# Forty-six of forty-eight input columns by seven block products, with heads that go through DRAM

## The chip, the core and the metric

The kernel runs on one core of a Trainium2 chip. The core has five engines that work side by side, each through its own queue of instructions in order: TensorE (PE in the profile) multiplies matrices, VectorE (DVE), ScalarE (ACT) and GpSimd (POOL) work element by element, and SyncE (SP) issues most of the DMA transfers. An instruction starts when the one ahead of it in its queue is done and the semaphores that it waits for have their values. The metric is the time in microseconds (us) of one execution on the device.

## What is computed

One layer of a hybrid encoder on 576 frames (512 of a prompt, 64 that continue a running stream of 512 cached frames), in float32, with 2048 channels:

```python
hn = rmsnorm(x, g_norm1)
q, k, v, gb, gc, hc = split(hn @ w_in)            # 2048 -> 6 x 1024 columns
q, k = rmsnorm(q per head, g_q), rmsnorm(k per head, g_k)
# attention, 8 heads x 128: A[t,s] = beta_ts * prod_{s<j<t}(1 - beta_tj), s < t
z = q @ k.T / sqrt(128)
log_1mb = where(s < t, log_sigmoid(-z), 0)
after = reversed_cumsum(log_1mb) - log_1mb
o_attn = where(s < t, exp(log_sigmoid(z) + after), 0) @ v
u = gc * hc                                       # convolution of width 3 along the frames
o_conv = gb * (w0*u[t-2] + w1*u[t-1] + w2*u[t])
x = x + concat(rmsnorm(o_attn, g_attn), rmsnorm(o_conv, g_conv)) @ w_out
h2 = rmsnorm(x, g_norm2)
x = x + (silu(h2 @ w_gate) * (h2 @ w_up)) @ w_down     # 2048 -> 5632 -> 2048
```

The normalised keys, the values and the last two rows of u are outputs too.

## The kernel before

Channels lie on the 128 partitions and frames along the free dimension, so every projection is a sum over 16 slices `k` of 128 channels of (128x128 weights) x (128x288 frames); the 576 frames are two halves of 288. Each operand is split in two float32r parts, hi and lo, and each slice takes three matmuls: hi x hi, lo x hi, hi x lo. ScalarE makes a hi part by a cast and VectorE the lo part by a subtraction; of 1024 columns of weights that is a pair of instructions (`split`, `weight_parts`).

A plain column chunk (128 of the 6144 columns of `w_in`) therefore takes 16 x 3 x 2 = 96 matmuls (`project`, `product`, tile "pj", L211). All 48 chunks are plain: three for each head (q, k, v), then three for each of the eight conv groups. x is transposed at the start into the tile `x_all` and also written to DRAM, since the residual needs it again.

For gate, up and down the kernel already uses the other scheme, a seven-product form of 2x2 block multiplication: a unit covers 256 columns by 2048 channels as blocks a11, a12, a21, a22, with the frames in blocks as well. `weight_sums` makes three sums and differences of weight blocks and `prepare` splits the operand of a product, four products ahead of its use, into one of four buffers `whl`. `run` does a product (24 matmuls over eight slices) and hands results on. A unit takes 7 x 24 = 168 matmuls where two plain chunks take 192.

Only PE's order is that in which the code is written; on the other engines a scheduler orders most instructions, except where the code asks for the written order (the start, and the last part). Small work on PE is interleaved by a queue of generators, `Pipeline`: a tick comes after each slice (three matmuls), and a generator that yields n is resumed n ticks later. So `attend`, the attention of a head, issues its pieces between slices of the projection that runs at the time, and a number behind `yield` says how much PE work lies between two pieces.

One head in `attend` is this chain. PE makes three blocks of scores z (the pieces z2, z1, z0) and the scores of the 64 sample frames against the cache (zs). ScalarE and VectorE form softplus of each block (three ScalarE activations and one VectorE instruction), GpSimd masks, and the result is split into hi and lo. PE then applies a triangular matrix to these parts (a cumulative sum) in z itself, and for the sample frames in the tile `cz`, from the split parts `sph` and `spl`; ScalarE takes exp; PE multiplies by v (tiles `po`, `os`). Before the change these pieces lie 15 to 18 ticks apart, and a head takes three chunks, 96 ticks.

After the heads and the conv groups `make_mix` normalises the two groups of channels, and the output projection follows, the attention half of `w_out` first, then the conv half with `after_b2`, which forms what the gate and up stage needs. Gate, up and down take up the rest of the time and are not touched by the change.

Of the kernel before, what the change touches and what calls it, by code (L numbers as in the profile page):

```python
# [16 lines left out]
P = 128  # L17
# [32 lines left out]
)  # L50

# [42 lines left out]
def tile_hybrid_stream_step(  # L94
# [21 lines left out]
    tmp = ctx.enter_context(tc.tile_pool(name="tmp", bufs=2, side="left"))  # L116

    lpad = ctx.enter_context(tc.tile_pool(name="lpad", bufs=1, side="left"))
    lpad.tile([P, 8], F32, name="lpad_t")
    rpad = ctx.enter_context(tc.tile_pool(name="rpad", bufs=1, side="right"))  # L120
    rpad.tile([P, 56], F32, name="rpad_t")
    acon = tc.alloc_tile_pool(name="acon", bufs=1, side="left")
    xt_dram = tc.dram_tile([KD, P, T], F32, name="xt_dram")
    x2_dram = tc.dram_tile([KD, P, T], F32, name="x2_dram")
    hid_dram = tc.dram_tile([NFP, 2 * FORMS, P, HALF], F32, name="hid_dram")
    ps_pj = ctx.enter_context(tc.tile_pool(name="ps_pj", bufs=3, space=PSUM))


    specs = []

    def col_chunk(w, col):
        specs.append((w[:, col : col + P].rearrange("(k p) c -> p k c", p=P), KD, P))

    for h in range(NH):
        for j in range(3):
            col_chunk(w_in, j * AW + h * P)
    for g in range(NG):
        for j in (1, 2, 0):
            col_chunk(w_in, 3 * AW + j * CW + g * P)
    for half in range(2):  # L140
        for c in range(D // 256):
            specs.append((w_out[half * AW : (half + 1) * AW, c * 256 : (c + 1) * 256]
                          .rearrange("(k p) c -> p k c", p=P), NH, 256))
# [5 lines left out]
    UNITS = [(kind, fp, 0, NP) for fp in range(1, NFP) for kind in ("gate", "up")]  # L149
    NGU = len(UNITS)  # L150
    calls = down_calls()
    UNITS += [("down", d, a, b - a) for d, a, b in DOWN]
# [37 lines left out]
    def next_weight():  # L190
# [5 lines left out]
        while len(ready) < min(i + 2, end):  # L196
            split_weight(nc.gpsimd if i == 2 else nc.vector)
# [8 lines left out]
    def half_of(x_, k, a, b):  # L206
        return x_[:, k, a // HALF, :] if len(x_.shape) == 4 else x_[:, k, a:b]

    def step(ps, whi, wlo, csl, xhi, xlo, k, nk, a, b):
        for n, (w_, x_) in enumerate(((whi, xhi), (wlo, xhi), (whi, xlo))):  # L210
            mm(ps, w_[:, k, csl], half_of(x_, k, a, b), start=(k == 0 and n == 0), stop=(k == nk - 1 and n == 2))  # L211

    def product(ps, whi, wlo, csl, xhi, xlo, nk, a, b):
        for k in range(nk):
            step(ps, whi, wlo, csl, xhi, xlo, k, nk, a, b)
# [6 lines left out]
    def parts(name):  # L222
        t = tmp.tile([P, 2, HALF], F32R, tag="hl", name=name)
        return t[:, 0], t[:, 1]
# [4 lines left out]
    onef = acon.tile([P, P], F32, name="onef")  # L229
    nc.vector.memset(onef, 1.0)  # L230
    oner = const.tile([P, P], F32R, name="oner")
    nc.vector.tensor_copy(oner, onef)
    neg1r = acon.tile([P, P], F32R, name="neg1r")
    nc.vector.tensor_scalar(out=neg1r, in0=onef, scalar1=-1.0, scalar2=None, op0=ALU.mult)
    neg1f = acon.tile([P, P], F32, name="neg1f")
    nc.vector.memset(neg1f, -1.0)
    trif = acon.tile([P, P], F32, name="trif")
    nc.gpsimd.affine_select(out=trif, in_=neg1f, compare_op=ALU.is_ge, fill=0.0, base=0,
                            pattern=[[-1, P]], channel_multiplier=1)
    trir = acon.tile([P, P], F32R, name="trir")  # L240
    nc.vector.tensor_copy(trir, trif)
    m01 = acon.tile([P, P], F32, name="m01")
    nc.gpsimd.affine_select(out=m01, in_=onef, compare_op=ALU.is_ge, fill=0.0, base=-1,
                            pattern=[[1, P]], channel_multiplier=-1)
    mneg = acon.tile([P, P], F32, name="mneg")
    nc.vector.tensor_scalar(out=mneg, in0=m01, scalar1=-NEG, scalar2=NEG, op0=ALU.mult, op1=ALU.add)
# [1152 lines left out]
```

## Time and profile before

| | us |
|---|---|
| median of three runs | 2439.27 (2436.69 to 2440.55) |
| the profiled execution: its own span | 2438.7 |
| PE busy | 2412.2 |
| DVE busy | 1736.5 |
| ACT busy | 1086.4 |
| POOL busy | 244.8 |

The profiled span is 0.6 us under the median, so no part of the time lies outside it that matters here. In lists of groups the columns are line, engine, operation, out<-in, shapes and count, then busy time and mean nanoseconds of one, then the idle time of the engine ahead of them and what ended it. A single matmul shows about twice its share, because two are in flight; what one costs is read from counts over a busy stretch. In timelines the columns are the start, the duration, and the instruction, with idle time ahead of it in brackets. In window tables each engine has its busy time and count, then come the clock granted to PE (1.00 is full), the share of DMA time and GB/s.

### The profile page before, as it was taken

To read this page: it belongs to the slowest core of one execution; us is meant where nothing else is said; L and a number is where in the kernel's file an instruction comes from. 1 tells how busy PE (TensorE), PEld (TensorE's weight loads), DVE (VectorE), ACT (ScalarE), POOL (GpSimd) and SP (SyncE) were. 2 spreads that over 40 slices of the span, in tenths; PEclk is the share of its full clock that TensorE was granted. 3 is DMA by queue.
4 is the path that set the end of the run, shared out by engine and by line. 5 is a ranking of instruction groups with operands and counts; after the bars stand their busy time and mean duration, and the time that the engine had idled before them with its cause. 6 is when DMAs were issued, how large, how long until landed. Compare 5 with 4: busy or idle time off the path is not lost.

```text
span 2438.7 us, 44038 instructions
## 1 busy us (share of the span) xinstructions
PE 2412.2 (99%) x18137; PEld 2403.7 (99%) x18137; DVE 1736.5 (71%) x2627; ACT 1086.4 (45%) x1929; POOL 244.8 (10%) x349
## 2 busy tenths in 40 slices
PE   8999999999999999999999999999999899999998
PEld 8999999999999999999999999999999899999998
DVE  7766666363335456888888888888888777887875
ACT  6655555241122245444444444444444444444454
POOL 2110101110010021000000000000000001431211
PEclk9999999999999999999999999999999999999999
DMA  8232232222234233443544444434544845885642
GB/s 263 85 102 84 76 92 78 82 84 85 79 93 155 97 125 100 148 152 114 159 151 131 140 143 148 144 122 154 156 127 144 310 153 171 240 233 193 202 126 79
DMA packets 464530, 336.49 MB, mean 138 GB/s; under 512 B 10191, under 2 KB 456521, under 8 KB 464329
## 3 DMA queue, kind: packets, MB, share of 16 engines
q1 hardware_dynamic: 459160, 326.90, 42.5%
q0 software_dynamic: 5168, 6.79, 1.5%
q8 instruction: 142, 2.33, 0.4%
q14 instruction: 60, 0.48, 0.1%
HBM read 269.33 MB, written 64.31 MB: 137 GB/s over the span
## 4 chain that ended last, share of the span: by engine, by line
PE 95%; DVE 2%; ACT 1%; DMA 0%; issue 0%; POOL 0%; SPq 0%; POOLq 0%; ACTq 0%; DVEq 0%
PE psy L1155 33%; PE pj L211 24%; PE psw L1155 17%; PE pjo L211 8%; PE psx L1155 8%; PE z L552 1%; PE pw L998 1%; PE po L618 1%; PE pot L1306 0%; PE os L648 0%; PE zs L578 0%; DVE whl L220 0%; DVE wlo L172 0%; ACT whi L171 0%; PE pjz L211 0%
## 5 line engine op out<-in xcount | busy, mean ns | idle before, releaser
L211 PE MATMUL pj<-x_all,whi 128*128 128x288 f32 x3008 | 627.0, 297 | 2.5 <-DVE x_all L347 1.7
L211 PEld LDWEIGHTS pj<-x_all,whi 128*128 128x128 f32 x3008 | 492.5, 189 | 3.6 <-DVE x_all L347 1.9
L211 PE MATMUL pj<-x_all,wlo 128*128 128x288 f32 x1504 | 444.9, 296 | 0.1
L1155 PE MATMUL psy<-t,whl 128*128 128x288 f32 x2916 | 438.6, 295 | 0.5 <-ACT part L1165 0.5
L1155 PE MATMUL psy<-h_s,whl 128*128 128x288 f32 x2724 | 411.5, 295 | 6.3 <-ACT part L1165 6.3
L1155 PEld LDWEIGHTS psy<-t,whl 128*128 128x128 f32 x2916 | 403.6, 189 | 0.9 <-ACT part L1165 0.7
L1155 PEld LDWEIGHTS psy<-h_s,whl 128*128 128x128 f32 x2724 | 378.6, 189 | 6.6 <-ACT part L1165 6.5
L1155 PE MATMUL psw<-t,whl 128*128 128x288 f32 x2592 | 377.1, 295 | 0.0
L1155 PEld LDWEIGHTS psw<-t,whl 128*128 128x128 f32 x2592 | 354.4, 189 | 0.2
L220 DVE TENSOR_TENSOR whl<-raw_a,whl 128x1024 fp32r<-128x1024 f32 (+4 forms) x288 | 309.5, 1075 | 61.5 <-ACT whl L219 60.1
L219 ACT CAST whl<-raw_a 128x1024 fp32r<-128x1024 f32 (+4 forms) x288 | 259.6, 902 | 109.8 <-issue 35.1
L211 PEld LDWEIGHTS pj<-x_all,wlo 128*128 128x128 f32 x1504 | 283.3, 188 | 0.8 <-DVE wlo L172 0.4
L220 DVE TENSOR_TENSOR whl<-raw_b,whl 128x1024 fp32r<-128x1024 f32 (+5 forms) x186 | 196.6, 1058 | 69.2 <-ACT whl L219 68.3
L171 ACT CAST whi<-raw_a 128x1024 fp32r<-128x1024 f32 (+1 forms) x138 | 140.1, 1031 | 233.3 <-PE pj L211 95.6
L219 ACT CAST whl<-raw_b 128x1024 fp32r<-128x1024 f32 (+5 forms) x186 | 161.1, 867 | 159.7 <-issue 69.8
L1165 ACT COPY part<-psy 128x288 f32<-128x288 f32 x237 | 94.8, 400 | 281.0 <-PE psy L1155 278.8
L172 DVE TENSOR_TENSOR wlo<-raw_a,whi 128x1024 fp32r<-128x1024 f32 (+1 forms) x132 | 160.9, 1231 | 25.6 <-ACT whi L171 24.3
L1155 PE MATMUL psx<-h_s,whl 128*128 128x288 f32 x1122 | 166.6, 296 | 2.3 <-DVE gs L978 2.3
L1155 PEld LDWEIGHTS psx<-h_s,whl 128*128 128x128 f32 x1122 | 155.7, 190 | 2.5 <-issue 2.5
L219 ACT CAST whl<-s 128x1024 fp32r<-128x1024 f32 (+5 forms) x79 | 70.1, 888 | 96.6 <-PE psw L1155 94.3
L941 POOL DMA_DIRECT2D hid_dram<-form x3 | 2.4, 807 | 922.6 <-DVE form L220 922.6
L220 DVE TENSOR_TENSOR whl<-s,whl 128x1024 fp32r<-128x1024 f32 (+5 forms) x79 | 80.6, 1020 | 14.7 <-ACT whl L219 14.4
(378 smaller groups left out, 3526.6 us busy)
## 6 DMA issues: line engine op xcount, KB each, us to landing
raw_a<-in_w_in_dram SPq DMA_DIRECT2D x47, 1024.0 KB, 5.5
hid_dram<-form SPq DMA_DIRECT2D x147, 288.0 KB, 2.3
raw_a<-in_w_gate_dram SPq DMA_DIRECT2D x23, 1024.0 KB, 5.7
raw_a<-in_w_up_dram SPq DMA_DIRECT2D x23, 1024.0 KB, 6.0
raw_b<-in_w_gate_dram SPq DMA_DIRECT2D x21, 1024.0 KB, 7.2
raw_b<-in_w_up_dram SPq DMA_DIRECT2D x21, 1024.0 KB, 6.6
h_s<-hid_dram SPq DMA_DIRECT2D x10, 2016.0 KB, 8.3
raw_a<-in_w_out_dram SPq DMA_DIRECT2D x16, 1024.0 KB, 5.2
```

The lines of the kernel that those rows point to most:

```text
L171: nc.scalar.copy(out=hi[:, a:b], in_=raw[:, a:b])
L172: lo_eng.tensor_tensor(out=lo[:, a:b], in0=raw[:, a:b], in1=hi[:, a:b].bitcast(F32), op=ALU.subtract)
L211: mm(ps, w_[:, k, csl], half_of(x_, k, a, b), start=(k == 0 and n == 0), stop=(k == nk - 1 and n == 2))
L219: nc.scalar.copy(out=hi, in_=src)
L220: (lo_eng or nc.vector).tensor_tensor(out=lo, in0=src, in1=hi.bitcast(F32), op=ALU.subtract)
L552: mm(zb[i], a_[:, kk], b_[:, q0:TP], start=(n == 0), stop=False, skip_group_check=True)
L618: mm(po[:, i * P : 512], a_[:, i, :], b_[:, : 512 - i * P], stop=(i == 0 and n == 2), **kw)
L941: q.dma_start(out=hid_dram[fp][2 * n - 2 : 2 * n].rearrange("f p t -> p f t"), in_=t.bitcast(F32))
L998: mm(pss[j, i], w_[:, k, j * P : (j + 1) * P], x_, start=(kk == 0 and k == 0 and n == 0), stop=(kk == 1 and k == 7 and n == 2))
L1155: mm(ps, whl[:, w_, j, :], x_, start=(start and j == 0 and q == 0), stop=(j == len(xs_) - 1 and q == 2), skip_group_check=True)
L1165: nc.scalar.copy(out=t, in_=st["y"])
```

## The change

The 48 chunks become one plain pair and 23 units of seven products (`HEADS_A`): eight units of gc and hc together, eight of q and k of one head, four of gb pairs, three of v pairs. The plain pair, v of heads 0 and 1, is multiplied while x arrives (`step0`).

- The start: `turn_x` writes all forms of x that the seven products need on chip (`b11`, `bod`, `b12a`), and `x_sums` and `x_rest` make the sums of blocks (`t12a`, `t34a`) for each pair of slices: two ScalarE scalings, three VectorE and one GpSimd difference, then two splits. The squares for the row scale R1 move from ScalarE and VectorE to GpSimd: `x_square` multiplies (the first eight slices) and adds (fifteen) in 576 columns.
- The units: `a_done` evacuates each quarter, multiplied by R1. `normed` normalises q and k with a second squaring and split per quarter and writes them to DRAM (`qk_dram`), `tokens` transposes k and v into token order (tiles `tok_a`, `tok_b`) ten or seven ticks after the last quarter. conv outputs go to DRAM as split parts (`mixc_dram`) and come back before the output projection.
- The conv half of the output projection now comes first, and all eight heads run beside it, one each 28 ticks (`PERIOD`) where there were 96; q, k, v of the next head are loaded from DRAM and split (`load_qk`, `load_v`). The yields of a head are 3, 3, 1, 8, 1, 2, 4, 3, 1, 3, 3.
- The norms of the two groups become a row scale after the product: `out_proj` has one more VectorE multiplication for each half of 288 frames.
- The attention half comes second, with `after_b2` beside it. The rest is as before.

```diff
+HEADS_A = (
+    ("gh", 0), ("gh", 1), ("qk", 0), ("gb", 0), ("qk", 1), ("gh", 2), ("qk", 2), ("gh", 3), ("qk", 3), ("gb", 1),
...
+NA = len(HEADS_A)
...
+    def x_sums(j, tag):
...
+        nc.vector.scalar_tensor_tensor(out=t1, in0=ev[:, HALF:], scalar=ge, in1=b11s, op0=ALU.mult, op1=ALU.subtract)
+        nc.gpsimd.tensor_tensor(out=t2, in0=b22s, in1=t1, op=ALU.subtract)
+        nc.vector.scalar_tensor_tensor(out=t3, in0=ev[:, HALF:], scalar=ge, in1=b22s, op0=ALU.mult, op1=ALU.subtract)
+        nc.vector.scalar_tensor_tensor(out=t4, in0=od[:, :HALF], scalar=go, in1=t2, op0=ALU.mult, op1=ALU.subtract)
+        two = t12a[j] = tpool.tile([P, 2, 2, HALF], F32R, tag=f"t{j}", name=f"t12a_{j}")
+        split(two[:, :, 0, :], two[:, :, 1, :], ta)
...
+    def x_square(kt, eng):
+        st = stp[kt // 2][:, kt % 2, :]
+        sq = accx if kt == 0 else lpool.tile([P, T + 2], F32, tag="c1", name="sqx")[:, :T]
+        if eng is nc.scalar:
+            eng.activation(out=sq, in_=st, func=AF.Square)
+        else:
+            eng.tensor_tensor(out=sq, in0=st, in1=st, op=ALU.mult)
+        if kt:
+            nc.gpsimd.tensor_tensor(out=accx, in0=accx, in1=sq, op=ALU.add)
...
+    def tokens(E, dst, dst_s, dram, lag):
+        yield lag
+        pa = misc("tok_a")
+        for i in range(4):
+            nc.tensor.transpose(pa[:, i * P : (i + 1) * P], E[:, i * P : (i + 1) * P], ident)
...
+    def normed(n, h, c, a, b, s2, E):
+        yield 13
+        ms = ss = channel_sums(s2[:, 0], s2[:, 1], a, b, "ss")
...
+        nc.vector.scalar_tensor_tensor(out=E[:, a:b], in0=E[:, a:b], scalar=col("gk") if c else gqs, in1=t,
+                                       op0=ALU.mult, op1=ALU.mult)
+        seen[n, c] = seen.get((n, c), 0) + 1
+        if seen[n, c] == 2:
+            nc.sync.dma_start(out=qk_dram[h, c], in_=E)
+            if c:
+                pipe.spawn(tokens(E, kp[:, h, :], ks[:, h, :], None, 10))
...
+        if (n, p_) == (-1, 3):
...
+            for g in range(NG):
+                nc.sync.dma_start(out=mixc[:, g].bitcast(F32), in_=mixc_dram[g])
...
+                    product(ps, whi, wlo, slice(j * P, (j + 1) * P), frame, 8, a, b)
+                    nc.vector.tensor_tensor(out=ps, in0=ps, in1=R[:, a:b], op=ALU.mult)
+                    nc.vector.tensor_tensor(out=x2(kt)[:, a:b], in0=ps, in1=x2(kt)[:, a:b], op=ALU.add)
...
+    def attend(h):
...
+        if h + 1 < NH:
+            load_qk(h + 1)
+        softplus(sp[:, :320], ws[:, TS:], sp[:, :320])
...
+        split(sph, spl, sp)
+        yield 8
+        if h + 1 < NH:
+            keys_cached()
+        yield 1
+
+        cz = misc("cz")
+        mm(cz[:, :320], trir, sph[:, :320], start=True, stop=False, skip_group_check=True)
...
+    PERIOD = 28
...
+        for h in range(NH):
+            pipe.spawn(attend(h))
+            yield PERIOD
```

Three places show how instructions moved. The first is GpSimd's queue at the start. Before, it holds parts of weight splits, the row scale and the first attention masks (`m_107` is the mask):

```order
L172 TENSOR_TENSOR wlo_146<-raw_a,whi_145 128x512 x3
L172 TENSOR_TENSOR wlo_174<-raw_a,whi_173 128x1024
L429 TENSOR_TENSOR rst<-ssr,nhalf 128x5
L749 MEMSET u 128x2
L751 COPY u<-vec 128x1 x2
L172 TENSOR_TENSOR wlo_690<-raw_a,whi_689 128x1024 x2
L561 TENSOR_TENSOR pr_953<-pr_953,m_107 128x128 x2
```

Now the squares (`sqx`, `accx`, 576 columns) of transposed slices `st` stand there, and the first difference `tab` of `x_sums` stands behind them. These are the last rows of that piece:

```order
L589 TENSOR_TENSOR sqx<-st_199 128x576
L591 TENSOR_TENSOR accx<-accx,sqx 128x576
L589 TENSOR_TENSOR sqx<-st_241 128x576
L591 TENSOR_TENSOR accx<-accx,sqx 128x576
L589 TENSOR_TENSOR sqx<-st_241 128x576
L591 TENSOR_TENSOR accx<-accx,sqx 128x576
L589 TENSOR_TENSOR sqx<-st_293 128x576
L591 TENSOR_TENSOR accx<-accx,sqx 128x576
L575 TENSOR_TENSOR tab<-b22s,tab 128x288
```

Thirteen instructions of 576 columns now stand ahead of the difference, on which the splits of `t12a` wait.

The second place is VectorE in the unit of q and k of head 2, up to the instruction that finishes k. Before, in the chunks of a head, k (`kf`, from `Ek`) was finished among these rows; `wlo` are weights of a later chunk:

```order
L506 TENSOR_TENSOR Ek<-pj,R_138 128x288
L172 TENSOR_TENSOR wlo_2477<-raw_a,whi_2476 128x1024
L451 TENSOR_TENSOR t<-y 128x288
L640 TENSOR_TENSOR ws<-cz,zc 128x320
L452 TENSOR_SCALAR t<-t,ms 128x288
L220 TENSOR_TENSOR sq<-sq 128x288
L453 TENSOR_SCALAR r<-t,y 128x288
L172 TENSOR_TENSOR wlo_2477<-raw_a,whi_2476 128x1024
L498 TENSOR_SCALAR kf<-Ek,vec,r 128x288
```

Now these are the rows ahead of the last scaling of k (`E-17_2499`; `E-17_2392` is q), which the four transposes `tok_a` on PE wait for:

```order
L755 TENSOR_SCALAR yt<-yt,ss 128x288
L809 TENSOR_TENSOR c<-c,R_681 128x288
L756 TENSOR_SCALAR yt<-yt 128x288
L341 TENSOR_TENSOR raw_b<-raw_b,raw_a 128x8x128
L757 TENSOR_SCALAR E-17_2392<-E-17_2392,gqs,yt 128x288
L343 TENSOR_TENSOR raw_a<-s_2808,raw_a 128x8x128
L755 TENSOR_SCALAR yt<-yt,ss 128x288
L223 TENSOR_TENSOR whl<-raw_a,whl 128x1024
L756 TENSOR_SCALAR yt<-yt 128x288
L223 TENSOR_TENSOR whl<-raw_b,whl 128x1024
L757 TENSOR_SCALAR E-17_2499<-E-17_2499,vec,yt 128x288
```

And on PE the transposes of k stand between the last slices of the product `psw` and the next product `psy`:

```order
L397 MATMUL psw<-t34a_705,whl 128x288 x3
L397 MATMUL psw<-t34a_736,whl 128x288 x3
L397 MATMUL psw<-t34a_778,whl 128x288 x3
L719 MATMUL tok_a<-ident,E-17_2499 128x128 x4
L397 MATMUL psy<-t12a_318,whl 128x288 x3
```

What moved is that sums and splits of weights, 1024 columns each, now stand between the steps of the norm, and that the transposes have become the next thing on PE behind the product whose end releases the operand buffer of the last `whl` row.

The third place is ScalarE in head 2 from the copy of the sample scores (`ws<-zs`) to the cast `sph`. Before, the samples' softplus (`sp`) had its own place late in the head:

```order
L526 ACTIVATE sp<-zc 128x320
L509 ACTIVATE sq<-Ek 128x288
L527 ACTIVATE sp<-sp 128x320
L219 COPY sq<-sq 128x288
L528 ACTIVATE sp<-sp 128x320
L219 COPY qh<-qf 128x224
L619 COPY o_attn<-po 128x512
L219 COPY sph<-sp 128x576
```

Now it stands among the softplus of the last block (`pr_6686`) and the casts of the next head's q and k (`hbl` holds the samples):

```order
L1065 COPY ws<-zs 128x320
L222 COPY s0h<-hbl 128x384
L993 ACTIVATE pr_6686<-pr_6686 128x512
L992 ACTIVATE hbl<-ws 128x320
L994 ACTIVATE pr_6686<-pr_6686 128x512
L222 COPY kh<-kf 128x512
L222 COPY qh<-qf 128x512
L993 ACTIVATE hbl<-hbl 128x320
L222 COPY ph_6688<-pr_6686 128x512
L994 ACTIVATE hbl<-hbl 128x320
L1022 COPY kcT<-kc 128x512
L222 COPY sph<-hbl 128x576
```

What moved is the distance: from the scores of z2 to `cz`, PE had 72 ticks of projection before, and has 16 ticks now.

1373 lines of the change are left out of this document (744 added, 629 removed).

## The prediction

> **What bounds the kernel now.** I read the page first (shares, the chain that ended last), then windows over the stages, then timelines of one head and of the two places where PE stood still.
>
> ```profile
> span 2438.7 us, 44038 instructions
> ...
> PE 2412.2 (99%) x18137; PEld 2403.7 (99%) x18137; DVE 1736.5 (71%) x2627; ACT 1086.4 (45%) x1929; POOL 244.8 (10%) x349
> ...
> PE 95%; DVE 2%; ACT 1%; DMA 0%; issue 0%; POOL 0%; SPq 0%; POOLq 0%; ACTq 0%; DVEq 0%
> ```
>
> PE is the bound nearly everywhere: of 2438.7 us it is idle for 26.5. A change is worth what it takes from PE, less each gap that it opens. The windows tell where the gaps are.
>
> ```profile
> 0.00:20.00 20.00, 14.11 (x71) 12.31 (x71) 12.22 (x28) 8.60 (x26) 2.82 (x11) 1.00 0.93 280
> 20.00:50.00 30.00, 28.32 (x218) 27.69 (x218) 23.86 (x46) 21.41 (x67) 8.17 (x7) 1.00 0.82 278
> 50.00:100.00 50.00, 48.37 (x359) 47.28 (x359) 37.74 (x78) 31.09 (x68) 8.74 (x11) 1.00 0.41 119
> 100.00:400.00 300.00, 299.32 (x2237) 296.81 (x2236) 191.65 (x374) 167.57 (x354) 35.07 (x76) 1.00 0.30 86
> 1000.00:1500.00 500.00, 499.51 (x3778) 499.27 (x3777) 419.57 (x570) 231.88 (x347) 0.00 (x0) 1.00 0.46 144
> ```
>
> ```profile
> 600.00:700.00 100.00, 100.00 (x758) 1.00 0.29 85
> ```
>
> The columns behind the length are PE, its weight loads, DVE, ACT, POOL, clock, DMA share, GB/s; the row by itself shows PE alone. The heads (100 to 400) keep PE full with ACT at 56% and DVE at 64%. The gate and up stage (1000 to 1500), which has the seven products already, keeps PE full with DVE at 84%. 758 matmuls of 288 columns in 100 us price one at 131.9 ns, 3778 in 499.5 at 132.2. Gaps lie at the start: 5.9 us in the first 20, 3.3 from 20 to 100.
>
> **What is removed.** 46 chunks of 96 matmuls become 23 units of 168, so 24 fewer per unit, 552 in all: 552 x 0.1319 = 72.8 us less PE work. Transposes, sums for norms and attention matmuls stay the same but for a few.
>
> **The start.** PE does 192 matmuls of the plain pair, then 136 of the first units, up to the transposes (tok_a) of v of head 0, which wait for R1: 328 x 0.1319 = 43, with about 84 transposes some 50 us. On the other engines the forms of x are new. Their prices:
>
> ```profile
> L172 DVE TENSOR_TENSOR wlo<-raw_a,whi 128x1024 fp32r<-128x1024 f32 x9 | 10.9, 1222 | 2.1 <-ACT whi L171 2.1
> L347 DVE SCALAR_TENSOR_TENSOR x_all<-o_attn,g1c,x_all 128x576 fp32r<-128x576 f32 x8 | 7.6, 954 | 0.3
> L346 DVE TENSOR_SCALAR x_all<-o_attn,g1c 128x576 fp32r<-128x576 f32 x8 | 4.1, 515 | 1.8 <-ACT o_attn L340 1.8
> L448 DVE TENSOR_SCALAR ms<-ss 128x288 f32<-128x288 f32 x8 | 3.6, 454 | 3.6 <-PE ss L458 3.6
> ```
>
> ```profile
> L172 POOL TENSOR_TENSOR wlo<-raw_a,whi 128x512 fp32r<-128x512 f32 x3 | 3.8, 1283 | 23.0 <-ACT whi L171 23.0
> ```
>
> VectorE alone, up to that transpose: 13 subtractions and 8 weight sums of 1024 (21 x 1.22 = 25.6), some 55 instructions of 288 (25.0), 8 x 0.95 and 8 x 0.52 (11.8), 16 splits of 576 (about 0.76, 12): 74 us, against 50 on PE. The chain is longer than that, because GpSimd paces it first. No row shows GpSimd at 576 columns; by 512 columns it is 1.28 x 576/512 = 1.44. Thirteen such instructions are 18.8 us, with what is ahead and the difference about 22; then ScalarE, in written order, holds the evacuations of later transposes behind the splits that wait for that difference, and three further rounds take 32 together, six more pairs of slices and the first splits 15, and VectorE's run up to R1 25: 94 us. Neighbours on one engine overlap by some 0.085 us (1.14 from start to start at 1024 columns, below), which takes about 6 off. So 88 against 50 is 38 late, where before lost 3.3. I take +30: the ends are +15 (VectorE's 74 less overlap is all that counts) and +40 (no overlap).
>
> **The units.** A unit's VectorE work is about 21 us (7 subtractions and 4 sums of 1024 are 13.4, the rest evacuations and norms) in 22.2 us of PE, so VectorE, not PE, is nearly the bound. Most waits are covered, since operands are prepared four products ahead. One isn't: in a unit of q and k the transposes of k stand directly behind the product psw; k's last scaling stands on VectorE behind a split of whl, whose cast can't start before psw ends and frees its buffer.
>
> ```profile
> 220.88 1.04 ACT L171 CAST whi<-raw_a 128x1024 fp32r<-128x1024 f32 x1
> ```
>
> ```profile
> 1007.85 1.22 DVE L1106 TENSOR_TENSOR raw_a<-raw_a 128x1024 f32<-128x1024 f32 x1
> 1008.98 1.22 DVE L220 TENSOR_TENSOR whl<-raw_a,whl 128x1024 fp32r<-128x1024 f32 x1
> 1011.09 0.46 DVE L978 TENSOR_TENSOR gs<-psw,part 128x288 f32<-128x288 f32 x1 [0.89 <-ACT part L1165]
> ```
>
> Cast 1.04, subtraction 1.22, scaling 0.46, two or three hand-overs: 2.9 us in which PE, whose next product stands behind the transposes, does nothing. Seven units of q and k: 20. In six of them a sum for a norm also waits some 0.7 for a split behind another (4), and the last two units, whose products follow one another closely, have about 5: together 29, ends 15 and 40 (VectorE itself late).
>
> **The clock.** A gap costs more than its length.
>
> ```profile
> 990.48 2.94 PE L1155 MATMUL psy<-h_s,whl 128*128 128x288 f32 x21
> ...
> 996.12 4.55 PE L1155 MATMUL psx<-h_s,whl 128*128 128x288 f32 x21 [2.31 <-DVE gs L978]
> ```
>
> ```profile
> 1920.00:1930.00 10.00, 4.50 (x35) 4.26 (x33) 6.79 (x15) 2.62 (x7) 2.69 (x4) 0.91 1.07 397
> 1930.00:1940.00 10.00, 9.19 (x55) 9.19 (x56) 7.37 (x14) 5.47 (x14) 0.96 (x2) 0.75 1.08 393
> ```
>
> After a gap of 2.31 us, 21 matmuls took 4.55 us where 2.94 is usual: 1.6 us lost. After the gap in 1920 to 1930 (6.3 us) 9.19 busy us held 55 matmuls, which are 7.25 at 0.132: 1.95 lost, at a granted clock of 0.75. The units' gaps of 2.9 are nearest to the first: 7 x 1.6 = 11, ends 0 and 14. The Trainium skill (TensorE: Matmul & The Clock Gate, Part 1: The HAM clock gate) has it that the clock is halved after an idle window of about 3.4 us, free-running. By that rule these gaps would keep the clock, and the sum would be 11 lower; the trace disagrees, with 2.31 us.
>
> **The heads.** Before, z and cz of a head are 38 us apart:
>
> ```profile
> 214.42 0.28 PE L552 MATMUL z<-qh,kh 128*128 128x256 f32 x1
> 216.44 1.06 PE L578 MATMUL zs<-qf,kcT 128*128 128x128 f32 x8
> ...
> 252.42 0.30 PE L634 MATMUL cz<-sph,trir 128*128 128x320 f32 x1
> ```
>
> Now PE has, from the end of z2 to cz: 16 ticks (48 matmuls, 6.3 us), z1 and z0, parts of po of the head before, zs and the transposes kc, together 10.2 us. Meanwhile ScalarE must do 25 instructions, in its queue's order:
>
> ```profile
> 215.19 0.49 ACT L526 ACTIVATE pr<-z 128x384 f32<-128x384 f32 x1 [3.43 <-PE z L549]
> ...
> 217.34 0.59 ACT L526 ACTIVATE pr<-z 128x512 f32<-128x512 f32 x1
> ...
> 218.24 0.40 ACT L219 CAST ph<-pr 128x256 fp32r<-128x256 f32 x1
> ...
> 223.72 0.62 ACT L219 CAST ph<-pr 128x512 fp32r<-128x512 f32 x1
> ...
> 244.04 0.47 ACT L528 ACTIVATE sp<-sp 128x320 f32<-128x320 f32 x1
> ...
> 244.97 0.49 DVE L529 SCALAR_TENSOR_TENSOR sp<-zc,sp 128x320 f32<-128x320 f32 x1
> ...
> 245.60 0.47 POOL L623 TENSOR_TENSOR sp<-sp,s 128x64 f32<-128x64 f32 x1 [9.31 <-DVE sp L529]
> ...
> 247.60 0.68 ACT L219 CAST sph<-sp 128x576 fp32r<-128x576 f32 x1 [1.65 <-POOL sp L629]
> ...
> 248.31 0.76 DVE L220 TENSOR_TENSOR spl<-sp,sph 128x576 fp32r<-128x576 f32 x1 [2.42 <-ACT sph L219]
> ```
>
> Nine of softplus of the blocks (six of 384 at 0.49, three of 512 at 0.6: 4.8), three of the samples (1.4), casts of ph, s1h, s0h (2.4), of q and k of the next head and its v (1.9), and the output and squares of the head before with the copy of zs (1.9): 12.4 us, with overlap about 11. From the end of the last activation (244.51) to the end of spl (249.07) are 4.6 more, over VectorE, GpSimd, ScalarE, VectorE in turn. So cz waits until 15.5 us where PE is there at 10.2: 5.3 us of gap, and a weight cast pair falls into the stretch in six of ten cases (+1.2). Six and a half per head, 52 for eight; ends 4 and 9 (ScalarE stands for GpSimd and for the loads of the next q and k). Ahead of the change nobody waited here. Each gap has the length of the one at 1920, so 8 x 1.95 = 16, ends 0 and 18. A head's second half (from cz on) gives PE 9.3 us and ScalarE 7, and keeps up.
>
> **What costs nothing.** One more VectorE multiplication per half in the output projection: 64 x 0.46 = 29 us beside 200 us of PE, with VectorE far from full; without that cover it would delay the accumulators. The stores of q, k, v and mix stand in SP's queue ahead of weight loads and wait there for their data; the loads are a unit ahead (22 us). mixc comes back, 4.7 MB, asked for six products (19 us) ahead of use; at the 280 GB/s of the first window that is 17 us, but the first w_out chunks and q, k share it. I take +2 for the entry of the conv half, ends 0 and 8.
>
> **Sum.** -72.8 + 30 + 29 + 11 + 52 + 16 + 2 = +67: 2438.7 + 67 = 2506. The profiled span stands 0.6 us under the median of the runs.
>
> **The rivals.** First, *faster*: the chains are shorter than their rows, as each instruction hides in its neighbours. All three chains are priced by durations; at a factor f the start's 94 us become 94f less 50 and 3, and the heads' 16.7 become 16.7f less 10.2. The timeline at 1008 shows 1.14 for 1.22 (0.93), at 288 columns it may be 0.82. The point of decision is near f = 0.75, where start (17), heads (18 and half the clock cost, 8) and units (20 and 9) just eat 72.8; at 0.65 the time would be 2406. Against it: steps that depend on each other showed no overlap (0.93 from 244.04 to 244.97). Second, *the clock stays full* in gaps under the page's window, and recovers sooner behind the others: 2506 - 27 = 2479, with one gap of 2.31 us against it. Third, *VectorE or a transfer is the bound* of the units: 21 of 22 us leave no room if the evacuations come in bursts; at 1.5 us more per unit and 8 at the entry 2506 + 35 + 6 = 2547. Fourth, the start's chain is hidden, as VectorE's work is all that counts and catches up in the conv units behind it: 2506 - 15 - 9 = 2482.
>
> **Chances.** Forecast (2490 to 2530) 0.50; clock or start milder (2455 to 2490) 0.22; VectorE or transfer bound (over 2530) 0.12; short chains 0.16, of which 0.13 faster by over 0.2%, 0.02 within it, the rest just slower. 0.2% (5 us) is about what runs of this kernel can tell from no change; its three spread by 3.9. The range 2440 to 2545 leaves out the faster cases and the worst of the third rival.
>
> **What would show it.** PE's busy time falls by about 73 less what a slower clock adds; the list of groups has idle time ahead of cz in the order of 50 us, released by VectorE's spl; tok_a about 20, released by VectorE's scaling; and the first tok_a, with the products behind the plain pair, some 35 in the first 100 us. The clock in the conv half reads about 0.8. Wrong would be a conv half of 28 ticks per head at 20 us a head: then ScalarE runs ahead of PE and the first rival holds.

## The result, and the profile after

The changed kernel takes 2566.11 us (median of four executions, 2565.22 to 2570.08) where the kernel before, beside it on the same chip, takes 2439.61. The ratio is 1.0524, with an interval of 1.0509 to 1.0539: slower, as forecast, but by 126.5 us where 67 were forecast, and 21 us above the top of the range.

The page of the profile after, its span, busy times and the chain that ended last by engine:

```profile
span 2564.7 us, 43686 instructions
...
PE 2394.8 (93%) x17579; PEld 2372.8 (93%) x17579; DVE 1976.3 (77%) x2800; ACT 1230.7 (48%) x2135; POOL 337.7 (13%) x407
...
PE 81%; DVE 9%; ACT 4%; POOL 2%; issue 2%; DMA 2%; SPq 0%; POOLq 0%; DVEq 0%; ACTq 0%
```

PE has 558 instructions less, yet its busy time fell by only 17.4 us, and its idle time rose from 26.5 to 169.9. With the 72.8 us that 552 matmuls cost at full clock, PE should have been busy for 2339.4; it was busy for 2394.8, and the 55.4 us more are nearly all matmuls at half clock, as the single microseconds below show. So -72.8 + 55.4 + 143.4 = +126.0, which is the difference of the spans. The windows say where: the start, the units of the input projection, the passage to the output projection, its conv half with the heads. First after, then the same times of before, which lie in other stages from 140 us on but show how full PE was there:

```profile
0.00:140.00 140.00, 95.81 (x586) 90.94 (x587) 111.73 (x137) 66.81 (x120) 57.74 (x50) 0.85 0.46 146
140.00:640.00 500.00, 469.13 (x3395) 464.74 (x3394) 392.42 (x510) 251.39 (x423) 66.88 (x72) 0.96 0.36 109
640.00:712.00 72.00, 59.86 (x424) 57.12 (x422) 44.30 (x76) 36.36 (x71) 3.82 (x9) 0.96 0.66 235
712.00:960.00 248.00, 181.90 (x1190) 174.24 (x1191) 135.70 (x268) 136.96 (x292) 56.56 (x108) 0.83 0.24 74
```

```profile
0.00:140.00 140.00, 130.11 (x937) 126.05 (x938) 98.75 (x197) 85.00 (x207) 24.14 (x39) 1.00 0.53 165
140.00:640.00 500.00, 500.00 (x3757) 497.68 (x3756) 275.82 (x518) 214.84 (x423) 54.34 (x116) 1.00 0.29 84
640.00:712.00 72.00, 72.00 (x547) 72.00 (x546) 26.35 (x40) 14.05 (x16) 2.15 (x11) 1.00 0.30 88
712.00:960.00 248.00, 248.00 (x1874) 247.97 (x1874) 131.36 (x217) 93.42 (x167) 42.61 (x49) 1.00 0.36 120
```

Length less PE's busy time gives the idle time: 44.2, 30.9, 12.1 and 66.1 us after, 9.9 in the first and none in the others before. Behind 960 us (834 before) the kernels are alike: PE is idle for 16.6 us in both. PE's timeline shows the kinds of gap, in brackets with what ended them:

```profile
89.14 6.10 PE L397 MATMUL psx<-bod,whl 128*128 128x288 f32 x24 [6.63 <-DVE c L806]
110.80 1.12 PE L719 MATMUL tok_a<-ident,E 128*128 128x128 f32 x4 [9.41 <-DVE E L700]
187.19 1.01 PE L719 MATMUL tok_a<-ident,E-21_1450 128*128 128x128 f32 x4 [2.34 <-DVE E-21_1450 L757]
238.72 1.11 PE L719 MATMUL tok_a<-ident,E-19_1981 128*128 128x128 f32 x4 [3.61 <-DVE E-19_1981 L757]
264.32 0.40 PE L278 MATMUL ss<-s,oner 128*128 128x288 f32 x1 [1.36 <-DVE s L792]
445.24 0.66 PE L719 MATMUL tok_a<-ident,E-11_4021 128*128 128x128 f32 x4 [3.61 <-DVE E-11_4021 L757]
714.85 1.08 PE L1021 MATMUL kc<-ident,cK 128*128 128x128 f32 x4 [7.61 <-DMA cK<-in_cache_k_dram]
873.94 0.63 PE L1082 MATMUL cz<-sph,trir 128*128 128x320 f32 x1 [9.53 <-ACT sph L222]
```

The group list sums those ahead of cz, once per head:

```profile
L1082 PE MATMUL cz<-sph,trir 128*128 128x320 f32 x8 | 5.1, 635 | 61.6 <-ACT sph L222 61.6
```

All the waits that the prediction named are there, each kind longer in sum: seven of tok_a with 2.3 to 3.6 us (21.8 in all), six sums for norms with 1.36, eight of cz with 5.1 to 9.7. Ahead of cz it is ScalarE's `sph` that ends them, not VectorE's `spl`, which the prediction named. One is new in size: the kc of head 1, where cached keys are transposed, 7.61 us.

The clock behind a gap, by single microseconds (the third column from the right):

```profile
187.00:188.00 1.00, 0.81 (x5) 0.81 (x6) 1.00 (x2) 0.00 (x0) 0.00 (x0) 0.68 0.39 130
188.00:189.00 1.00, 1.00 (x6) 1.00 (x6) 0.27 (x1) 0.59 (x1) 0.00 (x0) 0.50 0.73 205
...
191.00:192.00 1.00, 1.00 (x9) 1.00 (x9) 0.00 (x0) 0.00 (x0) 0.00 (x0) 1.00 1.14 380
```

Behind the gap of 2.34 us the clock is 0.50 and a microsecond holds 6 matmuls in place of 9 or 10. Summed over single microseconds (busy time by what the clock lacks to 1.00), the loss is 14.2 us in the start, 17.6 in the units, 1.6 in the passage and 18.9 in the heads: 52.2 of the 55.4, in 25 separate stretches. Fourteen of them are worth 1.5 to 1.7 us, nine of these in the units; the heads' eight average 2.4.

These stretches don't begin where a gap ends. From 14 us on, where the record of the clock begins, the trace has all 25 starting on one grid with steps of 3.41 us and lasting one to five whole steps. So it matters how the grid cuts a gap. The first two rows are steps around the gap of 3.61 us that ends at 238.72, the others around the one of 3.61 us that ends at 445.24:

```profile
235.14:238.55 3.41, 0.00 (x0) 0.00 (x0) 3.41 (x6) 1.04 (x1) 0.00 (x0) 1.00 0.31 108
238.55:241.97 3.42, 3.25 (x15) 3.24 (x15) 0.11 (x1) 0.59 (x1) 0.00 (x0) 0.50 1.06 327
439.94:443.35 3.41, 1.69 (x13) 1.46 (x12) 3.41 (x6) 1.60 (x3) 0.00 (x0) 1.00 0.23 87
443.35:446.77 3.42, 1.53 (x12) 1.53 (x13) 1.83 (x3) 0.58 (x1) 0.00 (x0) 1.00 0.68 184
446.77:450.18 3.41, 3.41 (x28) 3.41 (x27) 0.47 (x2) 1.20 (x3) 0.00 (x0) 1.00 1.06 327
```

The first gap fills a whole step, and the next step is at half clock; the second is cut into 1.7 and 1.9 us, and the clock stays full. In this execution each step at full clock in which PE was idle for more than 1.9 us was followed by one at half clock, and none with less than 1.49 us was. Between the two both occur, and what decides there is open.

### The profile page after: what moved, and what is told of

Read it like the earlier page. It is cut to its first block, busy times and chain, and to the rows that moved or that the text cites. A ratio compares the mean times of both kernels' runs of the same rounds, so it can differ in the third digit from the quotient of the medians.

```text
span 2564.7 us, 43686 instructions
## 1 busy us (share of the span) xinstructions
PE 2394.8 (93%) x17579; PEld 2372.8 (93%) x17579; DVE 1976.3 (77%) x2800; ACT 1230.7 (48%) x2135; POOL 337.7 (13%) x407
## 4 chain that ended last, share of the span: by engine, by line
PE 81%; DVE 9%; ACT 4%; POOL 2%; issue 2%; DMA 2%; SPq 0%; POOLq 0%; DVEq 0%; ACTq 0%
PE psy L397 41%; PE psw L397 20%; PE psx L397 10%; PE pjo L218 6%; DVE whl L223 2%; ACT whl L222 1%; DMA vtok<-v_dram 1%; DVE raw_b L341 1%; PE pw L1344 0%; DVE raw_a L343 0%; PE psv L397 0%; PE tok_a L719 0%; PE pot L1467 0%; DVE c L834 0%; POOL hbl L1073 0%
## 5 line engine op out<-in xcount | busy, mean ns | idle before, releaser
L223 DVE TENSOR_TENSOR whl<-raw_a,whl 128x1024 fp32r<-128x1024 f32 (+4 forms) x380 | 430.3, 1132 | 73.0 <-ACT whl L222 71.7
L222 ACT CAST whl<-raw_a 128x1024 fp32r<-128x1024 f32 (+4 forms) x380 | 356.4, 939 | 136.2 <-PE psx L397 46.1
L397 PE MATMUL psy<-t12a,whl 128*128 128x288 f32 x1104 | 174.8, 317 | 3.1 <-ACT part L420 3.1
L397 PEld LDWEIGHTS psy<-t12a,whl 128*128 128x128 f32 x1104 | 166.3, 208 | 4.3 <-ACT part L420 4.2
L397 PE MATMUL psw<-t34a,whl 128*128 128x288 f32 x1104 | 158.4, 298 | 4.1 <-DVE E-2_6454 L784 3.0
L397 PEld LDWEIGHTS psw<-t34a,whl 128*128 128x128 f32 x1104 | 151.9, 191 | 4.8 <-issue 3.2
L222 ACT CAST whl<-s 128x1024 fp32r<-128x1024 f32 (+4 forms) x102 | 94.3, 925 | 129.0 <-PE psw L397 122.6
L218 PE MATMUL pjo<-mixc,whi 128*128 128x288 f32 x512 | 127.8, 313 | 0.0
L223 DVE TENSOR_TENSOR whl<-s,whl 128x1024 fp32r<-128x1024 f32 (+4 forms) x102 | 108.6, 1064 | 20.9 <-ACT whl L222 19.0
L218 PE MATMUL pjo<-mixa,whi 128*128 128x288 f32 x512 | 102.1, 295 | 0.0
```

Source lines behind the costliest of these rows:

```text
L218: mm(ps, w_[:, k, csl], x_[:, a:b], start=(k == 0 and n == 0), stop=(k == nk - 1 and n == 2))
L222: nc.scalar.copy(out=hi, in_=src)
L223: (lo_eng or nc.vector).tensor_tensor(out=lo, in0=src, in1=hi.bitcast(F32), op=ALU.subtract)
L397: mm(ps, whl[:, w_, j, :], x_, start=(start and j == 0 and q == 0), stop=(j == len(xs_) - 1 and q == 2), skip_group_check=True)
```

## The experiments

Twelve kernels ran. The kernel before ran beside each group of them, at 2439.1 to 2440.0 us. Each ratio is to that kernel.

**The transposes of k, later.** The first theory is that of the prediction: PE waits at a few named instructions, each wait has its own cause, and the clock falls behind it.

```diff
-                pipe.spawn(tokens(E, kp[:, h, :], ks[:, h, :], None, 10))
+                pipe.spawn(tokens(E, kp[:, h, :], ks[:, h, :], None, 18))
```

> The transposes of k come 18 ticks after the last quarter in place of 10, so they no longer stand directly behind the product psw. Theory A (each gap costs its length and then a stretch at half clock): the seven gaps of 2.3 to 3.6 us (21.8 together) go, or shrink under the 1.4 us that left the clock alone, and with them 7 x 1.7 at half clock: 2566 - 33 = 2533, ratio to before 1.038. Theory B (only the idle time counts): 2566 - 21 = 2545. Theory C (VectorE's throughput bounds the units, so the wait turns up at another place): no more than 6 us less, 2560.

Measured: 2535.93, ratio 1.0403 (1.0388 to 1.0419). The same stage in the windows:

```profile
140.00:640.00 500.00, 483.42 (x3576) 478.91 (x3575) 411.75 (x536) 264.93 (x448) 65.42 (x74) 0.99 0.38 117
```

The time is nearest to Theory A. PE's idle time there falls from 30.9 to 16.6, of which 5.7 belong to the last units, which now lie in this window; the loss of clock falls from 17.6 to 6.7, and the gaps ahead of tok_a in these units are 0.4 us at most. The waits were a matter of place: k was asked for ten ticks behind its last quarter, before VectorE had worked through the sums and splits in between.

**Work in the gap ahead of cz.** Matmuls whose result is overwritten are put there, 414 in all, about as many as fill the wait. Work is added, nothing is taken away.

```diff
+        for i in range((32, 39, 48, 48, 57, 66, 67, 57)[h]):
+            mm(cz[:, :HALF], trir, mixc[:, i % NG, 0, :HALF], start=True, stop=True)
         mm(cz[:, :320], trir, sph[:, :320], start=True, stop=False, skip_group_check=True)
```

> Ahead of cz in each head PE does 32 to 67 further matmuls of 288 columns into the same bank, results overwritten: work added, sized to fill the wait of that head but for 0.8 us. The chain that cz waits for is as before. Theory A (half clock after each gap): the 18.9 us that the conv half loses to the clock fall to some 4: 2551. Theory B (PE is slow there for another reason, memory or ports): no gain, 2566 or a little more, and the granted clock of the conv half is as without.

Measured: 2552.76, ratio 1.0468 (1.0450 to 1.0485).

```profile
712.00:960.00 248.00, 237.97 (x1726) 231.81 (x1727) 149.70 (x293) 145.45 (x308) 59.75 (x111) 0.98 0.26 80
```

With 54.6 us of useless matmuls (414 x 0.1319) the kernel is 13 us faster. They stand in time that was idle, so they cost nothing, and the matmuls behind the gap run at full clock: the loss falls from 18.9 to 2.6. That measures the clock's share in the heads by itself. The whole gain, 13.4 us, is less than this fall of 16.3, since other stages of this execution lose a little more (1.2 us of idle time in the start, 1.6 of clock behind 960 us).

**cz later in the head.** The same gap, closed with the kernel's own work: cz goes behind the triangular products of the blocks and the first values, the splits of the next head's q and k go behind the samples' softplus, and the kc transposes behind a product.

```diff
-        yield 8
-        if h + 1 < NH:
-            keys_cached()
-        yield 1
-
-        cz = misc("cz")
...
+        values(2)
+        yield 2
+        cz = misc("cz")
...
+        values(1)
+        yield 3
+        values(0)
```

> cz moves behind the three triangular products and the first part of po, from tick 16 to tick 26 of a head, and the splits of the next head's q and k are issued at tick 18 in place of 7. Theory A (cz waits since its chain is 17 us long and PE comes after 10): the 63 us of idle time ahead of cz fall to under 20 and the clock's loss there from 19 to 8: 2510 to 2520. Theory C (ScalarE's 20 us per head bound the stage, whatever the order): the idle time moves to the triangular products, no more than 15 less, 2551.

Measured: 2501.51, ratio 1.0254 (1.0239 to 1.0269), better than expected.

```profile
712.00:960.00 248.00, 236.90 (x1682) 228.54 (x1682) 177.77 (x351) 163.47 (x350) 73.61 (x125) 0.97 0.32 104
```

Of 66.1 us idle 11.1 are left. ScalarE and VectorE had the time all along; what was lacking was PE work between the samples' scores and cz.

**The first transposes of v, later.** At the start the largest single gap is the one of 9.41 us ahead of the first tok_a. This run asks for them 24 ticks later.

```diff
-            pipe.spawn(tokens(e0[c], vp[:, c, :], vs[:, c, :], v_dram[c], 6 + 12 * c))
+            pipe.spawn(tokens(e0[c], vp[:, c, :], vs[:, c, :], v_dram[c], 30 + 12 * c))
```

> The first transposes that wait for R1 (v of heads 0 and 1) come 24 ticks later. Theory A1 (the 9.4 us ahead of them are that one wait): 9 less idle and 2 less at half clock, 2555. Theory A2 (VectorE has more work than PE up to there, so the next product waits for its operand in their place): 0 to 3 us less, 2564, with new idle time ahead of products within the next 20 us.

Measured: 2564.08, ratio 1.0516 (1.0500 to 1.0531): 2 us less, which the intervals can't tell from no change, as Theory A2 has it.

```profile
110.98 5.45 PE L397 MATMUL psy<-t12a,whl 128*128 128x288 f32 x24 [8.93 <-ACT part L420]
```

The wait moved to the next instruction that needs another engine. Unlike the gaps of the units, the start has no slack to give: something behind PE is late as a whole.

**Both of the first two repairs.** The edits are those of the later transposes of k and of cz.

> The transposes of k come 18 ticks behind their scaling (as in the run with later tokens), and cz comes later in the head (as in the run with cz behind the triangular products). Theory A: the two losses are separate places, each with its own gaps and clock, so the gains add: 2566.1 - 30.2 - 64.6 = 2471 (2467 to 2476). Theory B: both runs gave back the same wait at the entry of the conv half and the engines behind it are late in any case, so some of the gain is counted twice: 2477 to 2490.

Measured: 2471.46, ratio 1.0130 (1.0115 to 1.0145). The gains add to the microsecond (30.2 and 64.6 make 2471.3), so the two losses are separate.

**GpSimd out of the chain of t12a.** The prediction let GpSimd pace the start.

```diff
-        nc.gpsimd.tensor_tensor(out=t2, in0=b22s, in1=t1, op=ALU.subtract)
+        nc.vector.tensor_tensor(out=t2, in0=b22s, in1=t1, op=ALU.subtract)
```

> The difference t2 of x_sums goes from GpSimd, where it stands behind 13 squares and additions of 576 columns, to VectorE. Theory A, as in the prediction: GpSimd paces the start, so the first products of t12a and t34a start 10 to 15 us earlier and the time falls by as much, 2551 to 2556. Theory B: VectorE's own amount of work in the first 110 us is what PE waits for; GpSimd's place in the chain matters only for its first round, so 3 to 5 us fall off at the first gaps and reappear at the first tok_a: 2561 to 2566.

Measured: 2563.75, ratio 1.0511 (1.0495 to 1.0527): 2.4 us less, inside the 2561 to 2566 of Theory B and far from Theory A; the intervals overlap, so it may be no change at all.

```profile
107.73 1.12 PE L719 MATMUL tok_a<-ident,E 128*128 128x128 f32 x4 [10.26 <-DVE E L700]
```

All of the start comes 3 us earlier, and the first tok_a waits 0.9 longer. GpSimd's queue as a link of the chain was not what paced the start.

**The cached keys through another queue.** In SP's queue after, the load of cK for head 1 goes out at 709.89 us only, behind stores of v, one of which takes 6.15 us to issue, and behind loads of v, q and k:

```profile
695.39 6.15 SPq L723 DMA_DIRECT2D out_dram<-tok  x1
...
705.68 0.39 SPq L1013 DMA_DIRECT2D vtok<-v_dram  x1
...
709.89 0.42 SPq L924 DMA_DIRECT2D cK<-in_cache_k_dram  x1
```

```diff
-        nc.sync.dma_start(out=cK, in_=ck[:, h, :].rearrange("(i p) d -> p i d", p=P))
+        nc.gpsimd.dma_start(out=cK, in_=ck[:, h, :].rearrange("(i p) d -> p i d", p=P))
```

> The cached keys cK of a head are loaded through GpSimd's queue instead of SP's, where they stand behind a load that waits for stores. Theory A: the wait of 7.61 us ahead of the first kc is this queue; it falls under 2.5 us, and with the clock that it halves the time falls by 7 to 9: 2557 to 2559. Theory B: the transfer itself is late (bandwidth shared with mixc and w_out), the wait stays at 5 to 8 us and the time at 2564 to 2568.

Measured: 2561.77, ratio 1.0503 (1.0488 to 1.0519). The wait of kc is gone, so its place in SP's queue was the cause (the same store takes 6.67 us to issue there too), but only 4.3 us of it were gained, short of Theory A's 7 to 9: the next wait took the rest, the first cz (5.10 us in the change).

```profile
714.70 0.63 PE L1082 MATMUL cz<-sph,trir 128*128 128x320 f32 x1 [9.15 <-ACT sph L222]
```

**The small ones together.** Both repairs, t2 on VectorE, cK through GpSimd's queue, k's transposes at 16 ticks, the norm sums at 16 (13 before), and two products of the last units exchanged.

```diff
-        yield 13
+        yield 16
         ms = ss = channel_sums(s2[:, 0], s2[:, 1], a, b, "ss")
...
-              (-2, 7), (-2, 4), (-1, 6), (-1, 5), (-1, 7), (-1, 4)]
+              (-2, 7), (-1, 6), (-2, 4), (-1, 5), (-1, 7), (-1, 4)]
```

> cz later in the head, tokens of k 16 ticks behind, sums for the norms 16 ticks behind (13 before), the difference t2 on VectorE, cK through GpSimd's queue, and two products of the last two units exchanged. Theory A: each removes the wait that it is aimed at; sums 8 x .6, end of the units 5, entry 7 come on top of the other two changes: 2452 to 2460. Theory B: small waits turn into other small waits (ss at 16 and tokens at 16 stand close, VectorE has 21 of 22 us of work in a unit): 2465 to 2475. Neither ends below the kernel before: what is left is the start, some 34 us of gaps and 14 of clock.

Measured: 2449.80, ratio 1.0044 (1.0027 to 1.0060), a little better than expected. In the units 11.9 us of gaps are left and no loss of clock; of the 54.7 us left in the first 140 us, 42.1 are gaps and 12.6 clock.

**What makes the start late.** VectorE is busy for 92 of the 100 us from 10 to 110, so its own rows are what to look at. First GpSimd's, then VectorE's from the same time, and VectorE's from a time when GpSimd stands still, all of the change:

```profile
13.34 1.54 POOL L589 TENSOR_TENSOR sqx<-st 128x576 f32<-128x576 f32 x1
14.96 1.53 POOL L591 TENSOR_TENSOR accx<-accx,sqx 128x576 f32<-128x576 f32 x1
16.56 1.24 POOL L589 TENSOR_TENSOR sqx<-st 128x576 f32<-128x576 f32 x1
```

```profile
13.80 1.40 DVE L556 SCALAR_TENSOR_TENSOR b<-st,g1c,b 128x288 fp32r<-128x288 f32 x1
15.12 1.68 DVE L556 SCALAR_TENSOR_TENSOR b12a<-st,g1c,b12a 128x288 fp32r<-128x288 f32 x1
16.73 1.40 DVE L560 TENSOR_SCALAR bod<-st,g1c 128x576 fp32r<-128x576 f32 x1
...
47.03 0.51 DVE L556 SCALAR_TENSOR_TENSOR b12a<-st,g1c,b12a 128x288 fp32r<-128x288 f32 x1
47.49 0.52 DVE L560 TENSOR_SCALAR bod<-st,g1c 128x576 fp32r<-128x576 f32 x1
```

The same instruction takes 0.51 us alone and 1.40 to 1.68 beside GpSimd, and each long one ends shortly after an instruction of GpSimd does. Over all VectorE instructions from 5 to 115 us, each less the shortest of its line and shape, that is 24.6 us. So the squares for R1 were taken off GpSimd: ScalarE squares x in token order and sums along the row, as the kernel before does, and PE spreads the row scale (t2 stays on VectorE).

```diff
-            if kt < 8:
-                x_square(kt, nc.gpsimd)
+            if kt % 2 and kt < 10:
+                pair_squares(kt // 2)
...
+        nc.scalar.activation(out=src, in_=src, func=AF.Square, accum_out=ssx[:r, i, c : c + 1])
...
+            mm(psr[:, i * P : (i + 1) * P] if i < 4 else psr2[:, :TS], onef[:n, :], dgi[i], start=True, stop=True)
```

> The squares for R1 leave GpSimd: ScalarE squares x in token order with sums along the row (as the kernel before does), PE turns the row scale; the difference t2 is on VectorE, as in the run with t2 alone. GpSimd then does almost nothing in the first 100 us. Theory A: in the trace of the change, VectorE's instructions with two operands in SBUF or a scalar operand took 1.40 to 1.86 us where they overlap GpSimd's, and 0.51 to 0.82 elsewhere, 24.6 us too much in all up to 110 us; without GpSimd these go, VectorE needs some 80 us for the start in place of 105, PE's gaps in the first 140 us fall from 44 to some 25 and the clock's loss from 14 to some 8: 2541 (2534 to 2549). Theory B: the long durations are the forms' own, or ScalarE, which gets some 16 us more, is late in its place: 2556 to 2568.

Measured: 2551.60, ratio 1.0466 (1.0448 to 1.0483). 14.5 us less than the change and 12.2 less than with t2 alone, where the first theory gave 25 in all: the time lies between the two theories.

```profile
13.36 0.52 DVE L560 SCALAR_TENSOR_TENSOR b<-st,g1c,b 128x288 fp32r<-128x288 f32 x1 [1.38 <-ACT b L559]
13.80 0.51 DVE L560 SCALAR_TENSOR_TENSOR b12a<-st,g1c,b12a 128x288 fp32r<-128x288 f32 x1
14.87 0.52 DVE L564 TENSOR_SCALAR bod<-st,g1c 128x576 fp32r<-128x576 f32 x1 [0.56 <-ACT st L552]
```

```profile
31.29 0.67 ACT L222 CAST t34a<-tab 128x576 fp32r<-128x576 f32 x1 [5.96 <-DMA xt_dram<-st]
```

The durations are as short as the first theory has it; the excess falls from 24.6 to 1.0 us. VectorE now waits for others, and a wait comes to light that its lateness had covered: t34a takes the tile of x that is being stored to DRAM, and that store stands in SP's queue behind loads.

**The start on top of the small ones.** The same edit on the kernel with 2449.8.

> The same move of the squares on top of the version with all the smaller changes (2449.8). Theory A: the gain of the start adds, 2449.8 - 25 = 2425 (2417 to 2433), below the kernel before (2440). Theory B: 2440 to 2452.

Measured: 2439.08, ratio 0.9999 (0.9990 to 1.0009). 10.7 us are gained, again less than the 25 of the first theory, and the time equals that of the kernel before. Here the wait for the store is 7.89 us.

**The store earlier.**

```diff
             if kt == 6:
+                store_x(0)
                 load_vectors()
+                store_x(1)
```

> On top of c3: the stores of the first two pairs of x (xt_dram) stand in SP's queue ahead of the vectors and the weights of a later unit, where they stood behind them. In the trace of c3 ScalarE waited 7.89 us (from 25.3 to 33.2) with the first cast of t34a for that store, whose tile it takes over, and PE 8.64 us for ScalarE. Theory A: that wait goes, VectorE and ScalarE have slack behind it, and PE's gaps in the first 140 us fall from 34 to 25 or 26: 2439.1 - 9 = 2430 (2427 to 2433), below the kernel before. Theory B: VectorE's work from 60 to 98 us, where it is busy throughout, sets the first tok_a, and the wait reappears there: 2436 to 2440.

Measured: 2434.07, ratio 0.9977 (0.9968 to 0.9986).

```profile
26.87 0.67 ACT L222 CAST t34a<-tab 128x576 fp32r<-128x576 f32 x1 [1.52 <-DMA xt_dram<-st]
```

The wait falls to 1.52 us; of 6.4 us, 5.0 arrive at the end, a little short of the first theory.

**Some squares on VectorE.**

```diff
+        if 2 <= c <= 5 and i in (1, 3):
+            nc.vector.scalar_tensor_tensor(out=src, in0=src, scalar=1.0, in1=src, op0=ALU.mult, op1=ALU.mult,
+                                           accum_out=acc)
```

> As the version before it, and half of the squares of the pairs 1 to 4 on VectorE, which is idle a good third of the time from 10 to 55 us, instead of ScalarE, which PE waits for there (3.71 us at 45.8). Theory A: 2 to 4 us less than that version: 2427 (2424 to 2430). Theory B: the bound behind 60 us is VectorE, which gets 8 x 0.45 more: the same or 1 to 3 us more.

Measured: 2432.40, ratio 0.9969 (0.9958 to 0.9980). Not to be told from the run without it, since the intervals overlap; the first theory's 2430 is not reached.

```profile
PE 2363.6 (97%) x17585; PEld 2343.1 (96%) x17585; DVE 1953.0 (80%) x2825; ACT 1235.4 (51%) x2185; POOL 304.7 (13%) x385
```

With this span, 2435.6, the account is -72.8 + 24.2 (clock, 2363.6 less 2339.4) + 45.5 (idle, 72.0 less 26.5) = -3.1. This execution took the longest of the seven; by the medians the difference is -6.9. The idea of the change pays, by 0.2 to 0.3% (intervals 0.9958 to 0.9986 over the last two runs), once most of its waits are closed; the gaps and the lost clock of the first 140 us still come to 39 us (27.0 and 11.9).

## Why the prediction was wrong

| term | predicted | measured |
|---|---|---|
| matmuls | -72.8 | -72.8 at full clock |
| start, idle | +30 | +34.3 |
| units, idle | +29 | +38.3 |
| entry of the conv half, idle | +2 | +7.6 |
| heads, idle | +52 | +63.2 |
| clock | +27 | +55.4 |
| sum | +67 | +126.0 |

(Units: 30.9 up to 640 us and 7.4 of the next window. The entry's wait of 7.6 lies across 712 us, with 4.8 in that window and 2.9 in the heads' 66.1.) The direction and the places were right, and in the units and the heads the chains too, as the runs that close each place show. The sizes failed, all to the same side, and the largest miss is the clock. The time lies where the prediction had put 0.12, on a bound by VectorE or transfers in the units, but it got there by another way.

- **The clock.** The step that failed is "7 x 1.6" with "8 x 1.95". In the units the price of one loss was right, 1.5 to 1.7 us, and the gap of 2.31 us of the trace before foretold the one of 2.34; in the heads it was 2.4 in place of 1.95. The count was wrong: it took one loss for each gap of the units and the heads and none at the start, 15 in all; there were 25. Six lie in the start, worth 14.2 us, where the prediction had 30 us of gaps and no clock term, without a reason. The units up to the entry cost 19.2 in place of 11, since others follow gaps that it had put at 0.7 us: four of the six waits of 1.36 us for a norm sum are followed by a halved clock, as from 160 us on, two are not. The heads cost 18.9 in place of 16. (These are 52.2; the other 3.2 of the 55.4 are not placed.) By the rule of the Trainium skill that it weighed (TensorE: Matmul & The Clock Gate, Part 1: The HAM clock gate) these gaps would have kept the clock; the row of 188 us stands against the length of 3.4 us that the page gives, while the gap of 3.61 us that ends at 445.2 and costs nothing agrees with its free-running window, in which it matters where a gap falls, as the steps of 3.41 us do.
- **The heads.** "ScalarE must do 25 instructions", 11 us of them, with 1.2 for weight casts, was too little. In one head of the change ScalarE has 29 from 853.17 on, with two weight casts, and stands still for 3.9 us among them, mostly for GpSimd's masks:

```profile
853.17 0.22 ACT L1131 ACTIVATE sqa<-os 128x64 f32<-128x64 f32 x1 [0.74 <-DVE mixa L1127]
...
861.13 1.05 ACT L179 CAST whi<-raw_a 128x1024 fp32r<-128x1024 f32 x1
863.79 0.51 ACT L222 CAST ph<-hbl 128x384 fp32r<-128x384 f32 x1 [1.61 <-POOL hbl L1051]
...
868.24 1.03 ACT L179 CAST whi<-raw_a 128x1024 fp32r<-128x1024 f32 x1
...
870.01 0.47 ACT L994 ACTIVATE hbl<-hbl 128x320 f32<-128x320 f32 x1
873.21 0.67 ACT L222 CAST sph<-hbl 128x576 fp32r<-128x576 f32 x1 [2.73 <-POOL hbl L1073]
```

  The samples' softplus ends at 870.48, 17.3 us behind the first row, where about 12.2 were counted; most of the difference is the 3.9 us of standing still. The tail up to sph, 3.4 us, is no longer than in the trace of before. A chain priced by one engine's own work leaves out its waits for the other links.
- **The start.** +30 came out near 34.3, but by luck, since the reason was wrong. "GpSimd paces it first" fell with the run that took the difference off GpSimd: 2.4 us. The bound that the prediction set aside, VectorE's 74 us of work, was near the mark for the work itself (about 96 us busy up to the first tok_a, less 24.6, is 71). What it lacked is that GpSimd's squares make VectorE's instructions longer. The rows of before with which it priced `bod`, 0.95 and 0.52 us, were taken where GpSimd was busy for 14 to 27% of the time (2.82 of 20 us and 8.17 of 30); after, it is 57 and 59% of the same stretches (the fifth time in these windows of after):

```profile
0.00:20.00 20.00, 12.46 (x75) 11.51 (x75) 12.53 (x14) 10.29 (x21) 11.47 (x14) 1.00 0.91 288
20.00:50.00 30.00, 18.46 (x112) 17.20 (x113) 27.61 (x31) 13.78 (x29) 17.61 (x12) 0.84 0.43 151
```

  Its fourth rival, that VectorE's work is all that counts and catches up, had the right engine and the wrong length.
- **The units.** The waits of tok_a came to 21.8 us (20 predicted). The norm sums took 1.36 us each in place of 0.7, 8.2 in place of 4, and the last units 7.4 in place of 5.
- **The entry.** The +2, for mixc beside the first w_out chunks, looked at bytes; the wait was for order in SP's queue, 7.6 us.

The rivals: short chains fell, as the gaps of every stage came to more than forecast (single ones, three of tok_a and two of cz, were shorter). A full clock fell by the rows at 188 us. VectorE as the bound of the units fell with the later transposes, which took away most of that stage's gaps (30.9 to about 11 us) with VectorE's work unchanged.

## What to carry to other kernels

When several engines feed PE, price each gap twice: its length, and what the clock loses behind it. Here the second was 39% of the first (55.4 to 143.4), and gaps of 1.36 us took part. A saving in matmuls is kept only if every piece that waits for another engine has PE work in front of it, and moving two kinds of such pieces by some ticks was worth more here (30 and 65 us) than the matmuls that the change saves (73). Before small work goes to an idle GpSimd, look at whether VectorE works at the same time, in rows taken from such a time.

## What had not been expected of the hardware

- VectorE instructions lengthen beside GpSimd: 0.51 to 1.40 and 1.68 us at 288 columns, 0.82 to 1.86 for `bod` at 576. The Trainium skill (SBUF — State Buffer, Who interferes with whom) has it that a VectorE instruction with two operands in SBUF and a GpSimd instruction that reads SBUF share a port pair, and that the one that comes second waits until the first is done. The rows agree, and so does the run without the squares (excess 1.0 us). The row of 1.40 us for `bod` goes beyond that sentence: it has one tensor as operand, and a column of scalars.
- 414 matmuls whose results are overwritten made the kernel 13 us faster, since the clock behind the wait stayed up.
- A gap's length alone doesn't tell whether it costs clock: one of 2.34 us did, one of 3.61 did not, and of six of 1.36 four did. The halved stretches start on a fixed grid of 3.41 us, and the gap of 3.61 that cost nothing was cut by it into 1.7 and 1.9.
